# A hybrid attention layer on one core: attention cut into steps that a queue hands out between the pieces of the following projections, and nine instead of seven chunks of the first modulation piece on TensorE

## The chip, the cores and the metric

The kernel runs on one core of one Trainium2 chip. The time is device microseconds (us) for one execution of the whole program. Before the change it is 1295.29 us, the median of 3 runs (1293.72 to 1296.18). The profile comes from one further execution of the same program.

## What is computed

One decoder layer for 256 tokens of width 2048, all in fp32. Two attention branches run on the same normalised input `h`, and their outputs are gated and merged:

```python
mod = einsum('bd,de->be', silu(c), w_ada) + b_ada          # shift, scale, gate
h = rms_norm(x, g_pre) * (1 + scale) + shift
proj = einsum('bsd,de->bse', h, w_in)                      # 2048 -> 20032
q_mla, kv_a, z_mla, qkv_dil, z_dil, gl_mla, gl_dil = split(proj)
a = mla_branch(q_mla, kv_a, positions, g_kv, w_kv_b) * silu(z_mla)    # 16 heads, causal
bb = dilated_branch(qkv_dil, positions) * silu(z_dil)                 # 8 heads, 3 key groups
merged = sigmoid(gl_mla) * (a @ w_mla_proj) + sigmoid(gl_dil) * (bb @ w_dil_proj)
out = x + gate * rms_norm(merged @ w_o, g_post)
```

## The kernel before

**Projections.** Every projection is cut into column groups 512 wide (`group`, or `visit` for the first thirteen). A group walks the 2048 rows of its weight in chunks of 256 rows: `load_split` fetches a chunk of 512 KB into one of 8 `raw` buffers, ScalarE (ACT) casts it to a high part `whi`, VectorE (DVE) subtracts to get the low part `wlo` (4 buffers of each), and `multiply` issues 12 matmuls of 128x512 in fp32r: `whi` with the high part of `h`, `whi` with its low part, `wlo` with its high part, each for two rows of tiles and two token tiles. A whole group is 8 chunks.

**The head.** `h` can't be made before shift and scale are known. `ada_steps(0)` computes them for the first 384 channels out of 16 chunks of `w_ada`; `ROW_K` names the chunks that TensorE multiplies (into `row`, copied out by ACT, turned into columns by `pt_row`), the others are added up on DVE (tile `ada`, line L193). `keep_busy` issues matmuls into `idle`, whose result nobody reads. `finish` sums `ada` over the partitions (`pt_ada`), makes `colmul` and `colsh`, and calls `make_h`, which writes `hTh` and `hTl`, the high and low parts of `h`, for each 128 channels.

**Attention.** `dil_attention(quad)` treats 4 of the 8 dilated heads, one after the other; the body of the loop over `f`, `pr` and `h` treats the 16 latent heads. For each head: transposes of queries and keys on TensorE (`pt_qk`), copied out by ACT (`qk`); scores (`s_D`, `s_M`); mask and maximum on DVE, exponential on ACT (`sm`); transposes of the probabilities (`pt_p`), copied out by ACT (`pT`); the product with the values (`pv`); scaling on DVE. `transpose_split` then makes the operand of the next projection. In the code an attention stands as one block in front of the projections that follow it.

**What sets the order.** The code is traced, and a list scheduler fixes the order of each engine's instructions when the program is built; what stands earlier in the code has the higher priority, and where its inputs are not ready by the scheduler's own costs, later work is drawn ahead. So the projections behind an attention block already stand between its parts. On the chip every engine keeps that order and waits where an input is late. PSUM holds 2 accumulators and 4 smaller buffers (tag `b`) in these stages.

**In the trace,** an fp32 matmul that is no transpose stands as two instructions; a transpose and an fp32r matmul as one.

Of the kernel before, what the change touches and what calls it, by code (L numbers as in the profile page):

```python
# [9 lines left out]
F32 = mybir.dt.float32  # L10
F32R = mybir.dt.float32r
# [28 lines left out]
ROW_K = (1, 3, 5, 7, 9, 11, 13)  # L40
# [33 lines left out]
def hybrid_block(ctx: ExitStack, tc: tile.TileContext, x, c, positions, w_ada, b_ada, g_pre, g_post,  # L74
# [77 lines left out]
    def ada_steps(pi):  # L152
# [23 lines left out]
        def one(k0, kn):  # L176
# [23 lines left out]
        def finish():  # L200
# [12 lines left out]
            if pi == 0:  # L213
                keep_busy(acc[:, 0, :])
# [230 lines left out]

    def softmax(srcs, mask, n, scale, name):
# [39 lines left out]
    def dil_attention(quad):  # L486
        bb = slot([P, 2, 512], f"bb{quad}")
        for h in range(4):
            hs = slice(h * P, (h + 1) * P)
            nm = f"D{quad}{h}"  # L490
            qk = [qk_t([dil[0, g, quad][:, t, hs] for t in range(2)],
                       [dil[1, g, quad][:, t, hs] for t in range(2)], f"{nm}{g}") for g in range(3)]
            for t in range(2):
                nk = (t + 1) * P
                n = 3 * nk
                srcs = []
                for gs in ((0, 1, 2),) if t == 0 else ((0, 1), (2,)):
                    sc = tp_tile([P, len(gs) * nk], f"s_{nm}{t}{gs[0]}")
# [4 lines left out]
                sm, rl = softmax(srcs, md1 if t else md0, n, SC_DIL, f"{nm}{t}")  # L503
                pT = probs_t(sm, n // P, f"{nm}{t}")
                nb = 3 * (t + 1)
                pv = tp_tile([P, P], f"pv_{nm}{t}")
                for b in range(nb):
                    g, kt = divmod(b, t + 1)
                    T.matmul(pv, pT[:, b, :], dil[2, g, quad][:, kt, hs],  # L509
                             start=b == 0, stop=b == nb - 1)  # L510
                V.scalar_tensor_tensor(bb[:, t, hs], pv, rl, zd[quad][:, t, hs],
                                       op0=ALU.mult, op1=ALU.mult)
        bbT_h[quad] = slot([P, 4, S], f"bbTh{quad}", F32R)
        bbT_l[quad] = slot([P, 4, S], f"bbTl{quad}", F32R)
        transpose_split(bb, bbT_h[quad], bbT_l[quad], f"bb{quad}")
# [45 lines left out]
    for pi in range(len(PIECES)):  # L561
# [11 lines left out]
        for i, gi in enumerate(todo):  # L573
# [17 lines left out]
    for g in range(1, 3):  # L591
        for s in range(3):
# [3 lines left out]
            A.copy(dil[s, g, 1], acc)  # L596
    dil_rope(1)
    dil_attention(1)


    ssk = cp.tile([P, 2], F32, tag="ssk", name="ssk")
    for t in range(2):
        j = sp.tile([P, 768], F32, tag="sm", name=f"junk_kv{t}")
        A.activation(j[:, 0:512], kva[:, t, 0:512], AF.Square, accum_out=ssk[:, t:t + 1])
    rk = cp.tile([P, 2], F32, tag="rk", name="rk")
    rsqrt_mean(rk, ssk, 512, "rk")
    for t in range(2):
        V.tensor_scalar(kva[:, t, 0:512], kva[:, t, 0:512], rk[:, t:t + 1], None, op0=ALU.mult)
    ckv_h = slot([P, 4, S], "ckvh", F32R)
    ckv_l = slot([P, 4, S], "ckvl", F32R)  # L610
    for k in range(4):
        pt = tp_tile([P, 2, P], f"pt_ckv{k}")
        for t in range(2):
            T.transpose(pt[:, t, :], kva[:, t, k * P:(k + 1) * P], ident)
        h = sp.tile([P, S], F32, tag="h", bufs=H_BUFS, name=f"ckv{k}")
        V.tensor_scalar(h, pt.rearrange("p t n -> p (t n)"), gkv[:, k:k + 1], None, op0=ALU.mult)
        split(ckv_h[:, k, :], ckv_l[:, k, :], h)
    ckv = Opd([ckv_h], [ckv_l])

# [12 lines left out]
    V.memset(kz, 0.0)
    flat = pt.rearrange("p t n -> p (t n)")
    A.copy(kph, flat)
    for h in range(2):
        r, o = slice(h * 64, (h + 1) * 64), slice((1 - h) * 64, (2 - h) * 64)
        V.tensor_tensor(kpl[r, h, :], flat[r], kph[r].bitcast(F32), ALU.subtract)
        V.tensor_copy(kpl[o, h, :], kz[o])
# [4 lines left out]
    mqs, mq_done = {}, 0  # L643
    for f in range(4):
# [4 lines left out]
        for pr in range(2):  # L649
            j = 2 * f + pr  # L650
            gate_some(KC // UK // 2)
            while mq_done < 384 * (j + 1):
                acc = group(hT, win, KC, mq_done, 512, f"mq{mq_done // 512}")
                for i in range(mq_done // 384, (mq_done + 511) // 384 + 1):
# [9 lines left out]
            qp = sp.tile([P, 2, P], F32, tag="h", bufs=H_BUFS, name=f"qp{j}")  # L664
            rope(qp.rearrange("p t (h r) -> p (t h) r", r=64),
                 mq.rearrange("p t (h e) -> p (t h) e", e=192)[:, :, 128:192], cosMm, sinMm, 64, f"q{j}")
            pt = tp_tile([P, 2, P], f"pt_qp{j}")
            for t in range(2):
                T.transpose(pt[:, t, :], qp[:, t, :], ident)

            qst = sp.tile([P, 2, S], F32R, tag="qst", name=f"qst{j}")
            flat = pt.rearrange("p t n -> p (t n)")
            for h in range(2):
                r, o = slice(h * 64, (h + 1) * 64), slice((1 - h) * 64, (2 - h) * 64)
                A.copy(qst[r, h, :], flat[r])
                V.tensor_tensor(qst[o, h, :], flat[r], qst[r, h, :].bitcast(F32), ALU.subtract)
            for h in range(2):
                nm = f"M{j}{h}"
                qk = qk_t([mq[:, t, h * 192:h * 192 + P] for t in range(2)],
                          [kv[:, t, h * S:h * S + P] for t in range(2)], nm)  # L680
                sc = tp_tile([P, 3 * P], f"s_{nm}")
                for t in (1, 0):
                    nk = (t + 1) * P
                    o = 0 if t else S
                    T.matmul(sc[:, o:o + nk], qk[:, 0, t * P:(t + 1) * P], qk[:, 1, 0:nk],  # L685
                             start=True, stop=False)
                    qr = qst[:, h, t * P:(t + 1) * P]
                    T.matmul(sc[:, o:o + nk], qr, kph[:, 0:nk], start=False, stop=False)
                    T.matmul(sc[:, o:o + nk], qr, kpl[:, h, 0:nk], start=False, stop=True)
                sm = sp.tile([P, 768], F32, tag="sm", name=f"sm_{nm}")  # L690
                st = sp.tile([P, 8], F32, tag="stm", bufs=4, name=f"st_{nm}")
                for t in (1, 0):
                    nk = (t + 1) * P
                    o = 0 if t else S
                    V.tensor_tensor_reduce(sm[:, o:o + nk], sc[:, o:o + nk], mm[t], 1.0, -3e38,
                                           op0=ALU.add, op1=ALU.max, accum_out=st[:, t:t + 1])
                V.tensor_scalar(st[:, 2:4], st[:, 0:2], -SC_MLA, None, op0=ALU.mult)
                for t in (1, 0):
                    nk = (t + 1) * P
                    o = 0 if t else S  # L700
                    A.activation(sm[:, o:o + nk], sm[:, o:o + nk], AF.Exp, bias=st[:, 2 + t:3 + t], scale=SC_MLA,
                                 accum_out=st[:, 4 + t:5 + t])
                V.reciprocal(st[:, 6:8], st[:, 4:6])
                pT = probs_t(sm, 3, nm)
                pv = tp_tile([P, 2, P], f"pv_{nm}")
                vs = [kv[:, t, h * S + P:(h + 1) * S] for t in range(2)]
                T.matmul(pv[:, 1, :], pT[:, 0, :], vs[0], start=True, stop=False)
                T.matmul(pv[:, 1, :], pT[:, 1, :], vs[1], start=False, stop=True)
                T.matmul(pv[:, 0, :], pT[:, 2, :], vs[0], start=True, stop=True)
                hs = slice((2 * pr + h) * P, (2 * pr + h + 1) * P)  # L710
                for t in range(2):
# [107 lines left out]
```

## Time and profile before

| | |
|---|---|
| median of 3 runs | 1295.29 us (1293.72 to 1296.18) |
| the profiled execution's own time | 1292.55 us |
| its span in the trace | 1290.8 us |
| TensorE matmuls (PE) | busy 1265.4 us, 98% of the span, 6093 instructions |
| TensorE weight loads (PEld) | busy 1043.6 us, 81% |
| VectorE (DVE) | busy 821.1 us, 64% |
| ScalarE (ACT) | busy 601.0 us, 47% |
| DMA | 275 MB, mean 213 GB/s |

The stages, by the time from the span's start: the head to 36 us; the first thirteen groups in seven rounds to about 364 us; the attention of the first dilated quad (350 to 416 us) with six further groups behind it to 533 us; the attention of the second quad (to 590 us); the latent heads among their projections (590 to 902 us); gates and output projections to 1280 us; the tail. Matmuls are pipelined and their ends in the trace are modelled, so a start is read more surely than an end.

### The profile page before, as it was taken

To read this page: it belongs to the slowest core of one execution; us is meant where nothing else is said; L and a number is where in the kernel's file an instruction comes from. 1 tells how busy PE (TensorE), PEld (TensorE's weight loads), DVE (VectorE), ACT (ScalarE), POOL (GpSimd) and SP (SyncE) were. 2 spreads that over 40 slices of the span, in tenths; PEclk is the share of its full clock that TensorE was granted. 3 is DMA by queue.
4 is the path that set the end of the run, shared out by engine and by line. 5 is a ranking of instruction groups with operands and counts; after the bars stand their busy time and mean duration, and the time that the engine had idled before them with its cause. 6 is when DMAs were issued, how large, how long until landed. Compare 5 with 4: busy or idle time off the path is not lost.

```text
span 1290.8 us, 16449 instructions
## 1 busy us (share of the span) xinstructions
PE 1265.4 (98%) x6093; PEld 1043.6 (81%) x6093; DVE 821.1 (64%) x1203; ACT 601.0 (47%) x776; POOL 0.2 (0%) x4
## 2 busy tenths in 40 slices
PE   6999999999999999999999999999999999999997
PEld 3788888888888888888778888788888888888886
DVE  4888888896974445449666585675444444565545
ACT  3655334433365444455545555555444444433442
POOL 0000000000000000000000000000000000000000
PEclk9999999999999999999999999999999999999998
DMA  9999988986552766526768495674666666666751
GB/s 331 328 308 335 301 283 286 293 292 204 175 148 82 196 194 190 168 72 209 228 212 255 121 323 157 207 250 124 195 194 195 196 194 192 197 218 195 249 159 66
DMA packets 158172, 275.01 MB, mean 213 GB/s; under 512 B 9542, under 2 KB 46860, under 8 KB 158092
## 3 DMA queue, kind: packets, MB, share of 16 engines
q1 hardware_dynamic: 156276, 268.43, 66.5%
q10 hardware_dynamic: 1816, 5.53, 1.1%
q8 instruction: 48, 0.79, 0.2%
q14 instruction: 32, 0.26, 0.1%
HBM read 271.83 MB, written 2.10 MB: 212 GB/s over the span
## 4 chain that ended last, share of the span: by engine, by line
PE 94%; DVE 2%; DMA 1%; ACT 1%; issue 1%; DVEq 0%; SPq 0%; ACTq 0%
PE acc_d L264 30%; PE acc_mq L264 10%; PE acc_gd L264 7%; PE acc_ym L264 7%; PE acc_gm L264 7%; PE acc_zm L264 6%; PE acc_o L264 6%; PE acc_zd L264 3%; PE acc_yd L264 3%; PE acc_kv L264 3%; PE acc_kva L264 2%; PE pv_D L509 1%; PE s_D L500 1%; PE s_M L685 1%; PE pt_pD L466 1%
## 5 line engine op out<-in xcount | busy, mean ns | idle before, releaser
L253 ACT CAST whi_d<-raw_d 128x1024 fp32r<-128x1024 f32 (+1 forms) x156 | 152.8, 987 | 179.0 <-PE acc_d L264 145.3
L254 DVE TENSOR_TENSOR wlo_d<-raw_d,whi_d 128x1024 fp32r<-128x1024 f32 (+1 forms) x156 | 176.5, 1139 | 65.1 <-ACT whi_d L253 63.2
L264 PE MATMUL acc_d<-whi_d,hTl 128*128 128x512 f32 x576 | 159.4, 392 | 0.5 <-DVE hTl L231 0.5
L264 PE MATMUL acc_d<-whi_d,hTh 128*128 128x512 f32 x576 | 157.9, 392 | 1.4 <-DVE d L555 1.4
L264 PE MATMUL acc_d<-wlo_d,hTh 128*128 128x512 f32 x576 | 156.9, 390 | 0.0
L264 PEld LDWEIGHTS acc_d<-whi_d,hTh 128*128 128x128 f32 x576 | 107.2, 188 | 24.0 <-issue 1.8
L264 PEld LDWEIGHTS acc_d<-whi_d,hTl 128*128 128x128 f32 x576 | 107.8, 188 | 22.9 <-DVE hTl L231 1.0
L264 PEld LDWEIGHTS acc_d<-wlo_d,hTh 128*128 128x128 f32 x576 | 108.0, 188 | 22.3
L193 DVE SCALAR_TENSOR_TENSOR ada<-raw_a,ccol,ada 128x512 f32<-128x512 f32 (+1 forms) x98 | 79.4, 810 | 15.9 <-DMA raw_a<-in_w_ada 14.8
L254 DVE TENSOR_TENSOR wlo_mq<-raw_mq,whi_mq 128x1024 fp32r<-128x1024 f32 x48 | 58.6, 1222 | 24.4 <-ACT whi_mq L253 20.4
L253 ACT CAST whi_mq<-raw_mq 128x1024 fp32r<-128x1024 f32 x48 | 50.4, 1052 | 47.0 <-PE acc_mq L264 20.5
L254 DVE TENSOR_TENSOR wlo_gm<-raw_gm,whi_gm 128x1024 fp32r<-128x1024 f32 x32 | 39.2, 1225 | 45.4 <-ACT whi_gm L253 45.4
L254 DVE TENSOR_TENSOR wlo_gd<-raw_gd,whi_gd 128x1024 fp32r<-128x1024 f32 x32 | 39.2, 1224 | 32.4 <-ACT whi_gd L253 30.5
L254 DVE TENSOR_TENSOR wlo_ym<-raw_ym,whi_ym 128x1024 fp32r<-128x1024 f32 x32 | 39.1, 1223 | 32.1 <-ACT whi_ym L253 30.6
L253 ACT CAST whi_ym<-raw_ym 128x1024 fp32r<-128x1024 f32 x32 | 33.8, 1055 | 51.0 <-PE acc_ym L264 37.6
L253 ACT CAST whi_gm<-raw_gm 128x1024 fp32r<-128x1024 f32 x32 | 33.8, 1055 | 49.6 <-PE acc_gm L264 43.9
L254 DVE TENSOR_TENSOR wlo_o<-raw_o,whi_o 128x1024 fp32r<-128x1024 f32 x28 | 34.3, 1225 | 35.3 <-ACT whi_o L253 35.3
L264 PE MATMUL acc_mq<-wlo_mq,hTh 128*128 128x512 f32 x192 | 52.9, 393 | 0.0
L264 PE MATMUL acc_mq<-whi_mq,hTl 128*128 128x512 f32 x192 | 52.9, 394 | 0.0
L253 ACT CAST whi_gd<-raw_gd 128x1024 fp32r<-128x1024 f32 x32 | 33.7, 1053 | 40.5 <-PE acc_gd L264 20.4
L254 DVE TENSOR_TENSOR wlo_zm<-raw_zm,whi_zm 128x1024 fp32r<-128x1024 f32 x32 | 39.2, 1224 | 20.8 <-ACT whi_zm L253 18.2
L264 PE MATMUL acc_mq<-whi_mq,hTh 128*128 128x512 f32 x192 | 52.0, 392 | 0.0
(281 smaller groups left out, 2350.3 us busy)
## 6 DMA issues: line engine op xcount, KB each, us to landing
raw_d<-in_w_in SPq DMA_DIRECT2D x132, 512.0 KB, 4.6
raw_mq<-in_w_in SPq DMA_DIRECT2D x48, 512.0 KB, 4.6
raw_a<-in_w_ada SPq DMA_DIRECT2D x80, 256.0 KB, 4.7
raw_zm<-in_w_in SPq DMA_DIRECT2D x32, 512.0 KB, 4.4
raw_g<-in_w_ada SPq DMA_DIRECT2D x32, 512.0 KB, 4.2
raw_gd<-in_w_in SPq DMA_DIRECT2D x32, 512.0 KB, 4.4
raw_gm<-in_w_in SPq DMA_DIRECT2D x32, 512.0 KB, 3.8
raw_ym<-in_w_mla_proj SPq DMA_DIRECT2D x32, 512.0 KB, 3.7
```

The costliest lines, as they stand in the source:

```text
L193: V.scalar_tensor_tensor(flat, w, ccol[:, kk:kk + 1], flat, op0=ALU.mult, op1=ALU.add)
L253: A.copy(whi[:, :m], raw[:, :m])
L254: V.tensor_tensor(wlo[:, :m], raw[:, :m], whi[:, :m].bitcast(F32), ALU.subtract)
L264: T.matmul(acc[:, t, :n], opd.get(part, k0 + k, t), wt[:, k * n:(k + 1) * n], start=start and ph == 0 and k == 0, stop=stop and ph == 2 an ...
L466: T.transpose(pt[:, b, :], sm[:, (b0 + b) * P:(b0 + b + 1) * P], ident)
L500: T.matmul(sc[:, i * nk:(i + 1) * nk], qk[g][:, 0, t * P:(t + 1) * P], qk[g][:, 1, 0:nk], start=True, stop=True)
L509: T.matmul(pv, pT[:, b, :], dil[2, g, quad][:, kt, hs], start=b == 0, stop=b == nb - 1)
L685: T.matmul(sc[:, o:o + nk], qk[:, 0, t * P:(t + 1) * P], qk[:, 1, 0:nk], start=True, stop=False)
```

## The change

The attention functions become lists of closures. A list `side` holds them, and `run` takes one off (`tick`) after every chunk. `dil_steps` gives 16 steps for a quad (`s1` query and key transposes of a head, `s2` scores and softmax, `s3` probability transposes, `s4` the product with the values) in an order that overlaps neighbouring heads, and 2 steps for `transpose_split`; `kv_steps` gives 6 for the compressed keys, `mla_steps` 9 for two latent heads. What an instruction computes stays the same. In the head `ROW_K` has nine chunks instead of seven, `keep_busy` runs for chunks 12, 13 and 14 instead of 14 and 15, and the one in `finish` is gone.

```diff
-ROW_K = (1, 3, 5, 7, 9, 11, 13)
+ROW_K = (1, 2, 3, 5, 6, 7, 9, 10, 11)
...
-                if pi == 0 and kk > ROW_K[-1]:
+                if pi == 0 and ROW_K[-1] < kk < KC - 1:
                     keep_busy(v[:, k, 0, :])
...
                 make_h(a + lo, a + hi)
-            if pi == 0:
-                keep_busy(acc[:, 0, :])
...
+    side = []
+
+    def tick():
+        if side:
+            side.pop(0)()
+
     def run(acc, opd, w, a, b, c0, n, name):
 
         for k, kn in chunks(a, b, n):
             whi, wlo = load_split(w, k, kn, c0, n, f"{name}_{k}")
             multiply(acc, opd, whi, wlo, k, kn, n, k == a, k + kn == b)
+            tick()
...
-    def dil_attention(quad):
-        bb = slot([P, 2, 512], f"bb{quad}")
-        for h in range(4):
+    def dil_steps(quad):
+
+        bb = []
+        kept = {}
+
+        def s1(h):
...
+        def s3(h):
+            kept[h] = [(probs_t(sm, 3 * (t + 1), f"D{quad}{h}{t}"), rl) for t, (sm, rl) in enumerate(kept[h])]
...
+        order = [(s1, 0), (s2, 0), (s1, 1), (s3, 0), (s2, 1), (s4, 0), (s1, 2), (s3, 1), (s2, 2), (s4, 1),
+                 (s1, 3), (s3, 2), (s2, 3), (s4, 2), (s3, 3), (s4, 3)]
+        return ([lambda f=f, h=h: f(h) for f, h in order]
+                + transpose_steps(lambda: bb[0], bbT_h, bbT_l, quad, "bb"))
...
                 dil_rope(0)
-                dil_attention(0)
+                side.extend(dil_steps(0))
+                side.extend(kv_steps())
     A.activation(zd[1], zd[1], AF.Silu)
...
+    while side:
+        tick()
     dil_rope(1)
-    dil_attention(1)
...
+    side.extend(dil_steps(1))
...
+        return [rot] + [lambda f=f, h=h: f(h) for f in (s1, s2, s3, s4) for h in range(2)]
+
     for f in range(4):
...
+            side.extend(mla_steps(j, mq, kv, zm, av))
+        side.extend(transpose_steps(lambda av=av: av, aT_h, aT_l, f, "av"))
```

How this moves instructions is seen in the built programs. First TensorE in the attention of the first dilated quad, third head, before (`acc_d` is a projection, `pt_pD` the probability transposes, `pv_D` the product with the values, `s_D` the scores):

```order
L264 MATMUL acc_d_3598<-whi_d_2_3619,hTh_294 128x512 x4
L264 MATMUL acc_d_3598<-whi_d_2_3619,hTl_295 128x512
L466 MATMUL pt_pD_3310<-tid,sm_D_3303 128x128 x3
L264 MATMUL acc_d_3598<-whi_d_2_3619,hTl_295 128x512 x3
L509 MATMUL pv_D_3315<-d_205,pT_D_3309 128x128
L509 MATMUL pv_D_3315<-d_206,pT_D_3309 128x128
L509 MATMUL pv_D_3315<-d_207,pT_D_3309 128x128
L500 MATMUL s_D_3320<-qkD_3283 128x256
L500 MATMUL s_D_3320<-qkD_3290 128x256
L500 MATMUL s_D_3323<-qkD_3297 128x256
L264 MATMUL acc_d_3598<-wlo_d_2_3620,hTh_294 128x512 x4
```

The same place after the change, from the end of the chunk ahead of the probability transposes of that head:

```order
L262 MATMUL acc_d_3449<-wlo_d_6_3563,hTh_603 128x512 x4
L487 MATMUL pt_pD_3579<-tid,sm_D_3472 128x128 x3
L487 MATMUL pt_pD_3585<-tid,sm_D_3483 128x128 x3
L487 MATMUL pt_pD_3590<-tid,sm_D_3483 128x128 x3
L262 MATMUL acc_d_3449<-whi_d_8_3597,hTh_1458 128x512 x4
L262 MATMUL acc_d_3449<-whi_d_8_3597,hTl_1459 128x512 x4
L262 MATMUL acc_d_3449<-wlo_d_8_3598,hTh_1458 128x512 x4
L525 MATMUL s_D_3613<-qkD_3544 128x128
L525 MATMUL s_D_3613<-qkD_3551 128x128
L525 MATMUL s_D_3613<-qkD_3558 128x128
```

Three projection matmuls stood between the probability transposes and the product that needs them; now whole chunks of 12 stand between steps, and the step behind the transposes is another head's.

Then DVE in the head, before: the last three chunks that it adds up (`ada`), the two additions that wait for TensorE's row (`cols`, L173 and L174), and the first of the small operations behind them.

```order
L193 SCALAR_TENSOR_TENSOR ada_215<-raw_a_12_260,ccol,ada_215 128x768
L193 SCALAR_TENSOR_TENSOR ada_215<-raw_a_14_278,ccol,ada_215 128x768
L193 SCALAR_TENSOR_TENSOR ada_215<-raw_a_15_283,ccol,ada_215 128x768
L173 TENSOR_TENSOR cols<-cols,pt_row 128x3
L174 TENSOR_TENSOR cols<-cols,pt_row 128x3
L208 TENSOR_TENSOR adasc_288<-pt_ada_216,cols 128x1
```

After:

```order
L193 SCALAR_TENSOR_TENSOR ada_218<-raw_a_12_277,ccol,ada_218 128x768
L193 SCALAR_TENSOR_TENSOR ada_218<-raw_a_13_282,ccol,ada_218 128x768
L173 TENSOR_TENSOR cols<-cols,pt_row 128x3
L174 TENSOR_TENSOR cols<-cols,pt_row 128x3
L193 SCALAR_TENSOR_TENSOR ada_218<-raw_a_14_287,ccol,ada_218 128x768
L193 SCALAR_TENSOR_TENSOR ada_218<-raw_a_15_292,ccol,ada_218 128x768
```

The wait for the row now stands ahead of the last two chunks. A little further on the same queue, before:

```order
L211 TENSOR_TENSOR colsh<-pt_ada_216,cols 128x1
L231 SCALAR_TENSOR_TENSOR hTl_295<-h_296,colsh,hTh_294 128x256
L209 SCALAR_TENSOR_TENSOR colmul<-adasc_288,cols 128x1
L254 TENSOR_TENSOR wlo_d_0_326<-raw_d_0_323,whi_d_0_325 128x1024
L231 SCALAR_TENSOR_TENSOR hTl_295<-h_305,colsh,hTh_294 128x256
L229 SCALAR_TENSOR_TENSOR h_314<-xT_101,colmul,rstdT 128x256
```

After:

```order
L211 TENSOR_TENSOR colsh<-pt_ada_219,cols 128x1
L252 TENSOR_TENSOR wlo_d_0_331<-raw_d_0_328,whi_d_0_330 128x1024
L229 SCALAR_TENSOR_TENSOR hTl_302<-h_303,colsh,hTh_301 128x256
L229 SCALAR_TENSOR_TENSOR hTl_302<-h_312,colsh,hTh_301 128x256
L209 SCALAR_TENSOR_TENSOR colmul<-adasc_295,cols 128x1
L252 TENSOR_TENSOR wlo_d_2_349<-raw_d_2_346,whi_d_2_348 128x512
L227 SCALAR_TENSOR_TENSOR h_321<-xT_101,colmul,rstdT 128x256
```

Both weight splits (`wlo_d`) now stand ahead of the third `h`.

## Rows read from the trace of the kernel before

**Rows 1.** Stretch, length; busy (count) of PE, PEld, DVE, ACT, POOL; granted clock; DMA.

```profile
350.00:420.00 70.00, 69.81 (x399) 57.73 (x398) 43.52 (x90) 41.67 (x63) 0.00 (x0) 1.00 0.41 120
420.00:530.00 110.00, 110.00 (x487) 91.09 (x486) 57.25 (x70) 46.77 (x46) 0.00 (x0) 1.00 0.69 195
530.00:590.00 60.00, 59.75 (x349) 48.76 (x349) 28.83 (x80) 33.37 (x59) 0.00 (x0) 1.00 0.34 100
590.00:910.00 320.00, 317.42 (x1559) 260.90 (x1557) 211.15 (x358) 172.83 (x256) 0.00 (x0) 1.00 0.66 211
```

**Rows 2.** The same view of projection matmuls (L264) alone: PE, PEld, clock, DMA.

```profile
350.00:420.00 70.00, 46.69 (x187) 32.47 (x186) 1.00 0.41 120
530.00:590.00 60.00, 35.32 (x127) 22.45 (x127) 1.00 0.34 100
590.00:910.00 320.00, 283.19 (x1173) 215.97 (x1173) 1.00 0.66 211
```

**Rows 3.** Pieces of the chain that ended last: start us, us, what.

```profile
374.15 1.35 PE pv_D L509 x12
382.87 1.30 PE s_D L500 x6
...
1011.71 87.04 PE acc_gm L264 x384
...
1148.74 0.89 PE pt_m L442 x8
...
1269.69 5.78 PE acc_last L264 x48
```

**Rows 4.** Weight loads' longest wait, 530 to 910 us: total, times, longest.

```profile
PEld pt_pM L466 <- ACT sm_M L701: 4.8, 10, 1.3
```

**Rows 5.** Timeline of one dilated head's softmax: start, us, engine, line, operation.

```profile
382.71 1.46 PE L500 MATMUL s_D<-qkD 128*128 128x256 f32 x6
383.77 0.69 DVE L453 CUSTOM_DVE_ANT_0 sm_D<-s_D,msk 128x512 f32<-128x512 f32 x1 [0.51 <-PE s_D L500]
...
384.44 1.06 ACT L253 CAST whi_d<-raw_d 128x1024 fp32r<-128x1024 f32 x1 [2.55 <-PE acc_d L264]
...
386.55 0.82 PE L466 MATMUL pt_pD<-tid,sm_D 128*128 128x128 f32 x6
386.57 1.21 DVE L254 TENSOR_TENSOR wlo_d<-raw_d,whi_d 128x1024 fp32r<-128x1024 f32 x1
...
389.74 1.56 ACT L477 COPY qkD<-pt_qkD 128x512 f32<-128x512 f32 x3 [1.75 <-PE pt_qkD L475]
```

**Rows 6.** The page's costliest group of casts: busy, mean ns, idle before and what ended it.

```profile
L253 ACT CAST whi_d<-raw_d 128x1024 fp32r<-128x1024 f32 (+1 forms) x156 | 152.8, 987 | 179.0 <-PE acc_d L264 145.3
```

**Rows 7.** Timeline of the head.

```profile
25.50 1.45 PE L186 MATMUL row<-raw_a,ccol 128*1 128x384 f32 x4 [0.66 <-DMA raw_a<-in_w_ada]
...
26.60 2.07 DVE L193 SCALAR_TENSOR_TENSOR ada<-raw_a,ccol,ada 128x768 f32<-128x768 f32 x2 [1.09 <-DMA raw_a<-in_w_ada]
26.98 0.79 ACT L167 COPY rowp<-row 1x768 f32<-1x768 f32 x1 [13.15 <-PE row L186]
...
27.82 1.49 PE L171 MATMUL pt_row<-ones,rowp 1*128 1x1 f32 x12 [0.88 <-ACT rowp L167]
...
30.97 0.50 PE L206 MATMUL pt_ada<-ones,ada 128*128 128x1 f32 x4
...
31.33 0.89 PE L150 MATMUL idle<-ada,tid 128*128 128x384 f32 x2
...
35.66 0.48 DVE L229 SCALAR_TENSOR_TENSOR h<-xT,colmul,rstdT 128x256 f32<-128x256 f32 x1
35.79 0.73 PE L264 MATMUL acc_d<-whi_d,hTl 128*128 128x512 f32 x2 [0.52 <-DVE hTl L231]
...
36.17 0.51 ACT L230 ACTIVATE hTh<-h,colsh 128x256 fp32r<-128x256 f32 x1 [2.15 <-DVE h L229]
```

**Rows 8.** The view of Rows 1 behind the last matmul, which starts before 1281.3 us.

```profile
1284.00:1287.00 3.00, 0.00 (x0) 0.00 (x0) 2.77 (x4) 0.00 (x0) 0.00 (x0) 0.50 0.21 86
```

More of the change, by code (lines that the diff above doesn't have):

```diff
@@ L444, in transpose_split, with transpose_steps, step @@
             split(hi[:, 2 * hp:2 * hp + 2, :], lo[:, 2 * hp:2 * hp + 2, :], v)
+    def transpose_steps(src, dst_h, dst_l, i, name):
+        def step(hp):
+            if hp == 0:
+                dst_h[i] = slot([P, 4, S], f"{name}h{i}", F32R)
+                dst_l[i] = slot([P, 4, S], f"{name}l{i}", F32R)
+            pt = tp_tile([P, 2, 2, P], f"pt_{name}{i}{hp}")
+            for b in range(2):
+                for t in range(2):
+                    cc = (hp * 2 + b) * P
+                    T.transpose(pt[:, b, t, :], src()[:, t, cc:cc + P], ident)
+            v = pt.rearrange("p b t n -> p b (t n)")
+            split(dst_h[i][:, 2 * hp:2 * hp + 2, :], dst_l[i][:, 2 * hp:2 * hp + 2, :], v)
+        return [lambda hp=hp: step(hp) for hp in range(2)]
     def softmax(srcs, mask, n, scale, name):
@@ L502, in dil_attention, with s4 @@
                     srcs.append(sc)
-                sm, rl = softmax(srcs, md1 if t else md0, n, SC_DIL, f"{nm}{t}")
-                pT = probs_t(sm, n // P, f"{nm}{t}")
+                res.append(softmax(srcs, md1 if t else md0, 3 * nk, SC_DIL, f"D{quad}{h}{t}"))
+            kept[h] = res
+        def s3(h):
+            kept[h] = [(probs_t(sm, 3 * (t + 1), f"D{quad}{h}{t}"), rl) for t, (sm, rl) in enumerate(kept[h])]
+        def s4(h):
+            if not bb:
+                bb.append(slot([P, 2, 512], f"bb{quad}"))
+            hs = slice(h * P, (h + 1) * P)
+            for t, (pT, rl) in enumerate(kept[h]):
@@ L505, in dil_attention @@
                 nb = 3 * (t + 1)
-                pv = tp_tile([P, P], f"pv_{nm}{t}")
+                pv = tp_tile([P, P], f"pv_D{quad}{h}{t}")
                 for b in range(nb):
                     g, kt = divmod(b, t + 1)
[L509 to L512, printed above, removed]
@@ new lines, in dil_steps, with kv_steps, norm, turn @@
+        return ([lambda f=f, h=h: f(h) for f, h in order]
+                + transpose_steps(lambda: bb[0], bbT_h, bbT_l, quad, "bb"))
+    ckv_h, ckv_l = [], []
+    ckv = Opd(ckv_h, ckv_l)
+    kp = cp.tile([P, 2, P], F32, tag="kp", name="kp")
+    kph = cp.tile([P, S], F32R, tag="kph", name="kph")
+    kpl = cp.tile([P, 2, S], F32R, tag="kpl", name="kpl")
+    def kv_steps():
+        def norm():
+            ssk = cp.tile([P, 2], F32, tag="ssk", name="ssk")
+            junk = slot([P, 2, 512], "junk_kv")
+            for t in range(2):
+                A.activation(junk[:, t, :], kva[:, t, 0:512], AF.Square, accum_out=ssk[:, t:t + 1])
+            rk = cp.tile([P, 2], F32, tag="rk", name="rk")
+            rsqrt_mean(rk, ssk, 512, "rk")
+            for t in range(2):
+                V.tensor_scalar(kva[:, t, 0:512], kva[:, t, 0:512], rk[:, t:t + 1], None, op0=ALU.mult)
+                rope(kp[:, t:t + 1, 0:64], kpe[:, t:t + 1, :], cosM[:, t, 0:1, :], sinM[:, t, 0:1, :], 64, f"kp{t}")
+            V.tensor_copy(kp[:, :, 64:128], kp[:, :, 0:64])
+        def turn(k):
+            if k == 0:
+                ckv_h.append(slot([P, 4, S], "ckvh", F32R))
+                ckv_l.append(slot([P, 4, S], "ckvl", F32R))
+            pt = tp_tile([P, 2, P], f"pt_ckv{k}")
+            for t in range(2):
+                T.transpose(pt[:, t, :], kva[:, t, k * P:(k + 1) * P], ident)
+            h = sp.tile([P, S], F32, tag="h", bufs=H_BUFS, name=f"ckv{k}")
+            V.tensor_scalar(h, pt.rearrange("p t n -> p (t n)"), gkv[:, k:k + 1], None, op0=ALU.mult)
+            split(ckv_h[0][:, k, :], ckv_l[0][:, k, :], h)
+        def key():
+            pt = tp_tile([P, 2, P], "pt_kp")
+            for t in range(2):
+                T.transpose(pt[:, t, :], kp[:, t, :], ident)
+            kz = sp.tile([P, S], F32, tag="h", bufs=H_BUFS, name="kz")
+            V.memset(kz, 0.0)
+            flat = pt.rearrange("p t n -> p (t n)")
+            A.copy(kph, flat)
+            for h in range(2):
+                r, o = slice(h * 64, (h + 1) * 64), slice((1 - h) * 64, (2 - h) * 64)
+                V.tensor_tensor(kpl[r, h, :], flat[r], kph[r].bitcast(F32), ALU.subtract)
+                V.tensor_copy(kpl[o, h, :], kz[o])
+        return [norm] + [lambda k=k: turn(k) for k in range(4)] + [key]
@@ L663, in hybrid_block @@
             A.copy(kv, acc)
[L664 to L711, printed above, removed]
-                    V.scalar_tensor_tensor(av[:, t, hs], pv[:, t, :], st[:, 6 + t:7 + t], zm[:, t, hs],
-                                           op0=ALU.mult, op1=ALU.mult)
@@ L728, in hybrid_block @@
         part.append(sg)
+    while side:
+        tick()
     sgm = []
```

115 lines of the change are left out of this document (68 added, 47 removed).

## The prediction

> **What bounds the kernel now.** Start with the page's busy line: TensorE matmuls fill 98% of the span, VectorE 64%, ScalarE 47%. So TensorE is the bound, and the only time to be won without taking work away is time in which its work goes slower than it could. Busy time does not show that. In the stretch of the first quad's attention PE is busy 69.81 of 70 us, in one without attention 110.00 of 110 [rows 1]. So I count instructions and price them at the rate at which they run where nothing is waited for.
>
> The prices come from the chain, where a piece is printed with its length and count [rows 3]: 87.04 us for 384 projection matmuls 512 wide is 0.2267 each; 0.89 for 8 transposes is 0.111; 1.35 for 12 fp32 instructions 128 wide is 0.1125; 1.30 for 6 of 256 is 0.217; 5.78 for 48 fp32r ones 256 wide is 0.1204. Check: the 487 instructions between 420 and 530 us, all projections, cost 110.4 at 0.2267, and took 110.
>
> First quad, 350 to 420 us: 399 instructions, 187 of them projections [rows 1, 2]. The other 212 follow from the code: 92 transposes (48 for queries and keys, 36 for probabilities, 8 for `bb`), 96 fp32 instructions 128 wide, 24 of 256. Of the 187, 24 are the narrower `kva` (an estimate by their width: 0.134). The sum: 163 x 0.2267 = 36.95, 24 x 0.134 = 3.2, 92 x 0.111 = 10.2, 96 x 0.1125 = 10.8, 24 x 0.217 = 5.2, together 66.35. **3.7 us are lost.**
>
> Second quad, 530 to 590: 349 less 127 is 222 (the 212 and ten transposes of the compressed keys). 28.8 + 102 x 0.111 + 10.8 + 5.2 = 56.1 of 60. **3.9 lost.**
>
> Latent heads, 590 to 910: 1559 less 1173 is 386: 162 transposes (18.0), 96 for the values (10.8), 128 for the scores (32 each of fp32 256 and 128 wide, fp32r 256 and 128 wide: 6.9 + 3.6 + 3.9 + 3.6). With 1173 x 0.2267 = 265.9 that is 312.7 of 320. **7.3 lost.** Together 14.9 us, 1.2% of the time.
>
> What they are lost to stands among the waits: probability transposes wait for the exponential, 4.8 us in ten waits, the longest 1.3 [rows 4]. One case in full [rows 5]: scores issued from 382.71, the first maximum on DVE at 383.77, the transposes at 386.55. The scheduler had put only 11 projection matmuls (2.5 us) between scores and transposes, about the length of the chain, so any split of weights in the queues of DVE or ACT (1.2 and 1.06) shows as a wait.
>
> The Trainium skill (Perfetto Trace Analysis, Identifying the Most-Contended Engine) holds that matmul occupancy is a poor measure because the instructions are pipelined, and takes the busy share of weight loads in its place. The rows agree with its first half: 69.81 of 70 us busy hides 3.7 lost. By its second half the shares are 82.5, 81.3 and 81.5% in the three stretches against 82.8% between 420 and 530, and the loss would be 0.3 + 1.1 + 4.9 = 6.3 us, not 14.9. I go by the count, since the mix of sizes, not only waiting, moves that share.
>
> **The change, part by part.**
>
> *Attention as steps.* Nothing is added or taken away on TensorE, so its priced work is equal. What moves is the distance between a step and the one that needs its result. A chunk is 12 x 0.2267 = 2.72 us. In the built order of a quad, `s2` (scores) to `s3` (transposes) of a head is two chunks and the neighbour's `s1`: 5.4 + 1.3 = 6.8 us. The chain that must fit is the 2.5 us of [rows 5]; with two splits of 1.2 ahead of it on DVE it is 5.0. `s3` to `s4` is two chunks and an `s2`, 7.4 us, against copies of about 0.5 each. `s1` to `s2` is the tightest, one chunk of 2.7 against three copies (1.56) behind one cast (1.06): 2.6. The last `s3` to `s4` of a quad also has one chunk. Among the latent heads each such pair has at least one chunk and mostly two (5.4 us) against a maximum, an exponential and one split. So nearly every wait named above loses its reason. What stays: ten one-chunk places at about 0.1, and the change between kinds of matmul at some 120 places, which at 0.02 (within the price of a transpose, so not measured alone) is 2.4. I take 3.4 us as staying, 11.5 won. Bounds: all 14.9 from above; from below nothing, since each engine's queue could bring the waits back.
>
> *The splits.* A step's copies and exponentials stand in ACT's and DVE's queues before the casts and splits of later chunks, and TensorE waits for those. Cover: ACT's casts are held up by TensorE's release of the four buffers (145.3 of 179.0 us of idle time ahead of `whi_d`, [rows 6]), so they run about three chunks, 8 us, ahead. Load: at a chunk and a step every 4.3 us DVE has a split and by my estimate about 0.8 of attention (a maximum takes 0.69), ACT a cast and about 1.2 (copies of 0.52) [rows 5]. I cost it at nothing. Without that cover the price would be what a step holds the queue, 1 to 2 us.
>
> *The compressed keys' steps* move from the second quad's end to the groups before it: ten transposes, 1.1 us, unchanged in price, and DVE's small operations into a stretch where it is busy 57 of 110 us [rows 1]. Nothing.
>
> *Nine chunks.* [rows 7] give the head before: the last `row` chunk starts at 25.50 and takes 1.45, its copy 0.79 at 26.98, `pt_row` 27.82, two idle matmul pairs, `pt_ada` at 30.97, though DVE has its last chunk added at 28.67. After: a chunk of `row` costs about 1.3 on TensorE and the chunks land about 1.05 apart (both estimates: four matmuls take 1.45, and DVE adds two chunks in 2.07 as they land), so I put the end of the ninth near 25.4; the copy ends near 26.3, `pt_row` near 27.9, 1.3 earlier. Three idle pairs of 0.9 follow instead of two (1.72 for two), so `pt_ada` comes near 30.6, 0.4 earlier. DVE now has the wait for `pt_row` ahead of its last two chunks: 28.2 + 2 x 1.02 = 30.3 instead of 28.67, just in time. The pair taken out of `finish` (31.33) frees perhaps 0.2. Against it: both weight splits (1.2 and 0.7) now stand ahead of the third `h` on DVE; it starts near 36.1 instead of 35.66, its cast ends near 37.2, and the first projection needs it there at 37.15 before the change. The sum is 0.1 to the bad, which I take as 0. Bounds: 0.9 won (0.4 + 0.2 and an `h` that is in time), 1.2 lost (one split in the open).
>
> **Sum.** 1292.55 (the profiled execution) - 11.5 + 0 = 1281.05. The median of the runs lies 2.74 above that execution, so 1283.8, say **1284 us**.
>
> **The rivals.**
>
> *Only part comes back.* The short waits of 0.1 to 0.2 may belong to the change of kinds rather than to late inputs; then only those above half a microsecond go, and 4 to 7 us are won: 1288 to 1291. For it: most of the ten waits behind 4.8 us are short [rows 4]. Against: they are named with a releaser. By the skill's measure above it would be 1289. Chance 0.18.
>
> *No change.* The scheduler already fills the gaps, the new order meets its waits in the queues of DVE instead, and 1294 to 1297 is measured. Against: the distances above are twice the chain. Chance 0.06.
>
> *Slower: the splits come late.* ACT and DVE keep their order, so an exponential that stands there waiting for its maximum holds up the casts behind it. One cast late beyond its 8 us stops TensorE. It decides from 0.6 us for each of the 24 heads (14.9 / 24); at 1 us a head the time is 1295 + 24 - 15 = 1304. For it: DVE in the latent stretch is busy 211 of 320 us and has its gate sums there. Against: [rows 6]. Chance 0.05.
>
> *Slower by the clock.* With one idle pair gone TensorE could stand still long enough in the head to lose its clock; behind the last matmul it is granted 0.50 [rows 8], against 1.00 everywhere else after the head's start. A few us of projections at 1.2 instead of 2.4 GHz cost about 2. It alone would not turn the sign: 1286. Chance 0.03, within the forecast's range. The skill (TensorE: Matmul & The Clock Gate, Why this matters for your kernels) warns of gaps between bursts of matmuls in the same sense.
>
> **How the numbers follow.** Forecast 0.71 with its own range 1280.5 to 1287.5; part 0.18; none 0.06; slower 0.05. The range that leaves out two in ten: 1280 (all of 14.9 and a little of the head) to 1290.5, in the middle of the part case. About 0.2% (2.6 us) is what a measurement can tell from no change: faster 0.88, same 0.07, slower 0.05.
>
> **What would show it.** Right: between 350 and 910 us the same count takes about 11 us less; the wait of `pt_pM` for `sm_M` is gone from the list; whole chunks of 12 stand between steps in the timeline; the first full run of projections starts within 1 us of 36; no waits of projections for `whi` or `wlo`. Wrong: such waits appear, or the lost time in the three stretches stays above 8 us, or the granted clock is below 1.00 in the head.

## The result and the profile after

The change takes 1281.49 us (median of 4 executions, 1280.25 to 1282.87), the kernel before 1294.97 (4 executions, 1293.72 to 1296.18): a ratio of 0.9897, 95% interval 0.9885 to 0.9910. The profiled execution of the change took 1281.44 us with a span of 1279.7, 11.1 below the span of before.

Where the 11.1 us came from is read between marks that both kernels have: the one transpose `pt_pos` of the last round, and the first matmul of `acc_ym`. Timeline of PE before (start, us, engine, line, operation):

```profile
323.34 0.22 PE L376 MATMUL pt_pos<-tid,posf 2*128 2x2 f32 x1
1098.58 1.07 PE L264 MATMUL acc_ym<-whi_ym,aTh 128*128 128x512 f32 x4
```

The same of the change:

```profile
324.99 0.22 PE L382 MATMUL pt_pos<-tid,posf 2*128 2x2 f32 x1
1087.48 1.07 PE L262 MATMUL acc_ym<-whi_ym,avh 128*128 128x512 f32 x4
```

Between the marks, where all attention lies, 775.24 us became 762.49: **12.75 won**. Up to the first mark the change is **1.65 later**. Behind the second nothing changed (192.2 us to the end of the span in both). 12.75 - 1.65 = 11.1.

**The attention.** The stretches of [rows 1] after the change (same columns):

```profile
350.00:420.00 70.00, 70.00 (x402) 60.87 (x401) 45.98 (x100) 41.30 (x63) 0.00 (x0) 1.00 0.49 139
590.00:910.00 320.00, 320.00 (x1602) 268.69 (x1601) 196.98 (x340) 172.98 (x257) 0.00 (x0) 1.00 0.66 202
```

PE starts 43 more instructions in the same 320 us (1559 before). The waits of PE's weight loads before, from 340 to 930 us, beside [rows 4] (total us, times, longest):

```profile
PEld pv_D L509 <- ACT pT_D L467: 5.1, 15, 0.4
...
PEld pt_pD L466 <- ACT sm_D L457: 4.5, 15, 0.4
PEld s_M L685 <- ACT qkM L477: 2.5, 14, 0.2
...
PEld s_M L688 <- DVE qst L676: 1.8, 3, 1.3
```

All nine groups of that list make 25.3 us, more than the 12.75 won, so a listed wait is not lost time in full. After the change one is left in the same stretch:

```profile
PEld s_D L525 <- ACT qkD L498: 0.2, 1, 0.2
```

It stands at 361.94 us, in the first head, where one chunk lies between the copies and the scores: the place that the prediction called the tightest.

The timeline of the third head's scores shows why, beside [rows 5]:

```profile
389.67 2.13 PE L525 MATMUL s_D<-qkD 128*128 128x128 f32 x12
390.09 1.22 DVE L252 TENSOR_TENSOR wlo_d<-raw_d,whi_d 128x1024 fp32r<-128x1024 f32 x1 [1.60 <-ACT whi_d L251]
391.24 0.55 DVE L474 CUSTOM_DVE_ANT_0 sm_D<-s_D,msk 128x384 f32<-128x384 f32 x1
391.45 1.28 PE L262 MATMUL acc_d<-whi_d,hTh 128*128 128x512 f32 x4
...
393.33 0.94 ACT L478 ACTIVATE sm_D<-sm_D,st_D 128x768 f32<-128x768 f32 x1
393.48 1.08 PE L262 MATMUL acc_d<-wlo_d,hTh 128*128 128x512 f32 x4
...
394.40 2.17 PE L543 MATMUL pv_D<-d,pT_D 128*128 128x128 f32 x18
...
396.32 1.17 PE L262 MATMUL acc_d<-whi_d,hTh 128*128 128x512 f32 x4
...
397.34 0.85 PE L262 MATMUL acc_d<-whi_d,hTl 128*128 128x512 f32 x3
```

While DVE and ACT work on this head (391.24 to 394.3), PE multiplies a whole chunk and then the values of the second head; a split of 1.22 us ahead of the maximum delays nothing.

**The head.** Here the granted clock fell. Windows of the change (length; PE, PEld, DVE, ACT, POOL; granted clock; DMA):

```profile
27.00:28.00 1.00, 1.00 (x10) 0.98 (x10) 0.00 (x0) 0.00 (x0) 0.00 (x0) 0.91 1.04 385
28.00:31.00 3.00, 2.94 (x5) 1.33 (x5) 2.17 (x4) 1.04 (x1) 0.00 (x0) 0.50 1.08 356
31.00:32.00 1.00, 1.00 (x6) 0.60 (x4) 0.00 (x0) 0.00 (x0) 0.00 (x0) 0.88 1.06 330
32.00:34.00 2.00, 1.37 (x12) 1.20 (x11) 1.51 (x8) 0.51 (x1) 0.00 (x0) 1.00 0.93 289
34.00:35.00 1.00, 0.99 (x5) 0.56 (x5) 0.95 (x4) 0.80 (x2) 0.00 (x0) 0.82 1.05 346
35.00:38.00 3.00, 2.96 (x7) 1.85 (x8) 2.43 (x6) 0.75 (x3) 0.00 (x0) 0.50 0.97 320
```

The profiled execution of before has 1.00 throughout:

```profile
27.00:40.00 13.00, 11.27 (x55) 8.34 (x56) 9.50 (x24) 5.96 (x9) 0.00 (x0) 1.00 0.96 324
```

Timeline of the change at the same place, against [rows 7]:

```profile
25.67 0.79 ACT L167 COPY rowp<-row 1x768 f32<-1x768 f32 x1 [11.82 <-PE row L186]
26.51 1.54 PE L171 MATMUL pt_row<-ones,rowp 1*128 1x1 f32 x12 [0.88 <-ACT rowp L167]
27.98 4.01 PE L150 MATMUL idle<-raw_a,tid 128*128 128x384 f32 x6
28.23 2.07 DVE L193 SCALAR_TENSOR_TENSOR ada<-raw_a,ccol,ada 128x768 f32<-128x768 f32 x2
31.84 0.50 PE L206 MATMUL pt_ada<-ones,ada 128*128 128x1 f32 x4
36.95 0.48 DVE L227 SCALAR_TENSOR_TENSOR h<-xT,colmul,rstdT 128x256 f32<-128x256 f32 x1
```

DVE's sum is ready at 30.30, as forecast; but behind a wait of 0.88 and twelve tiny matmuls the clock falls to 0.50 (1.2 GHz), the six idle matmuls take 4.01 us instead of the 2.7 forecast, and `pt_ada`, queued behind them, comes at 31.84 instead of 30.6. Behind the small matmuls of `pt_ada` it falls again, from 34.8 to 38 us, under the first projections.

### The profile page after: what moved, and what is told of

Its sections match the earlier page's. It is cut to its first block, busy times and chain, and to the rows that moved or that the text cites. A ratio compares the mean times of both kernels' runs of the same rounds, so it can differ in the third digit from the quotient of the medians.

```text
span 1279.7 us, 16445 instructions
## 1 busy us (share of the span) xinstructions
PE 1260.7 (99%) x6101; PEld 1050.0 (82%) x6101; DVE 814.8 (64%) x1201; ACT 601.9 (47%) x778; POOL 0.2 (0%) x4
## 4 chain that ended last, share of the span: by engine, by line
PE 98%; DVE 1%; DMA 0%; ACT 0%; issue 0%; DVEq 0%; SPq 0%; ACTq 0%
PE acc_d L262 31%; PE acc_mq L262 10%; PE acc_zm L262 7%; PE acc_gd L262 7%; PE acc_ym L262 7%; PE acc_gm L262 7%; PE acc_o L262 6%; PE acc_kv L262 3%; PE acc_yd L262 3%; PE acc_zd L262 3%; PE acc_kva L262 2%; PE pv_D L543 1%; PE s_D L525 1%; PE s_M L722 1%; PE row L186 1%; PE pt_pD L487 1%
## 5 line engine op out<-in xcount | busy, mean ns | idle before, releaser
L252 DVE TENSOR_TENSOR wlo_gd<-raw_gd,whi_gd 128x1024 fp32r<-128x1024 f32 x32 | 39.2, 1224 | 37.3 <-ACT whi_gd L251 37.3
L262 PE MATMUL acc_mq<-whi_mq,hTh 128*128 128x512 f32 x192 | 55.2, 409 | 0.0
L251 ACT CAST whi_zm<-raw_zm 128x1024 fp32r<-128x1024 f32 x32 | 33.6, 1051 | 39.5 <-PE acc_zm L262 12.5
```

What stands on the lines that cost most here:

```text
L251: A.copy(whi[:, :m], raw[:, :m])
L252: V.tensor_tensor(wlo[:, :m], raw[:, :m], whi[:, :m].bitcast(F32), ALU.subtract)
L262: T.matmul(acc[:, t, :n], opd.get(part, k0 + k, t), wt[:, k * n:(k + 1) * n], start=start and ph == 0 and k == 0, stop=stop and ph == 2 an ...
```

## The experiments

"Stretch" is the time between the two marks. The expectations count it from an earlier mark, which adds 105.3 us in every kernel. The clock is the mean granted clock over an execution. Before was run again beside each; its medians there were 1295.57, 1293.57, 1295.36 and 1295.90.

| kernel | stretch, us | median, us (range; executions) | mean clock | ratio to before, interval |
|---|---|---|---|---|
| before | 775.24 | 1295.36 (1292.45 to 1298.50; 17) | 0.992 to 0.998 | |
| the change | 762.49 | 1281.49 (1280.25 to 1282.87; 4) | 0.995 to 0.996 | 0.9897 [0.9885, 0.9910] |
| head alone | 775.62 | 1294.28 (1292.44 to 1295.48; 12) | 0.994 to 0.997 | 0.9995 [0.9985, 1.0004] |
| steps alone | 762.56 | 1279.90 (1279.78 to 1283.44; 5) | 0.994 to 0.998 | 0.9896 [0.9880, 0.9912] |
| in order | 763.74 | 1283.78 (1282.93 to 1285.17; 4) | 0.992 to 0.995 | 0.9913 [0.9896, 0.9930] |
| two per chunk | 762.43 | 1280.50 (1279.95 to 1284.20; 4) | 0.993 to 0.997 | 0.9896 [0.9879, 0.9913] |
| no idle | 762.59 | 1281.81 (1281.21 to 1282.14; 5) | 0.994 to 0.995 | 0.9910 [0.9894, 0.9926] |
| steps, fill | 762.55 | 1280.18 (1279.93 to 1280.31; 4) | 0.997 to 0.998 | 0.9898 [0.9882, 0.9913] |
| change, fill | 762.58 | 1280.10 (1279.95 to 1280.81; 4) | 0.997 to 0.998 | 0.9898 [0.9883, 0.9914] |
| two buffers | 763.31 | 1290.94 (1288.73 to 1293.97; 10) | 0.993 to 0.996 | 0.9977 [0.9963, 0.9990] |
| at once | 784.81 | 1303.21 (1302.98 to 1305.08; 4) | 0.988 to 0.991 | 1.0059 [1.0044, 1.0073] |
| half chunks | 771.56 | 1290.80 (1289.32 to 1292.01; 6) | 0.994 to 0.997 | 0.9964 [0.9950, 0.9978] |
| before, fill | 774.79 | 1292.73 (1292.24 to 1294.22; 11) | 0.997 to 0.998 | 0.9982 [0.9972, 0.9992] |
| at once, late kv | 769.11 | 1288.92 (1288.49 to 1290.29; 5) | 0.993 to 0.995 | 0.9948 [0.9931, 0.9965] |

**The two halves of the change.** The head alone, in the kernel before:

```diff
-ROW_K = (1, 3, 5, 7, 9, 11, 13)
+ROW_K = (1, 2, 3, 5, 6, 7, 9, 10, 11)
-                if pi == 0 and kk > ROW_K[-1]:
+                if pi == 0 and ROW_K[-1] < kk < KC - 1:
-            if pi == 0:
-                keep_busy(acc[:, 0, :])
```

> The kernel before with the head of the change alone: nine chunks of the row on TensorE, idle matmuls at chunks 12, 13 and 14, none in finish. The prediction (head costs 0, bounds 0.9 won and 1.2 lost): the time of before within 0.5 us. Rival, read from the trace of the change (probability sums delayed from 30.97 to 31.84 us behind three idle pairs, second low part of h from 35.26 to 35.9 behind a weight split): 1.0 to 1.6 us slower than before, with the same losses as before in the attention stretches.

The steps alone, which is the change with these lines put back:

> The change with the head of before: seven chunks, idle matmuls at chunks 14 and 15 and in finish, all attention still handed out step by step. If the head of the change costs nothing, the time is that of the change within 0.5 us. If it costs 1.0 to 1.6 us, this kernel is faster than the change by that much: about 1280.1 us, a span of 1278.4, some 12.4 below the span of before.

The stretch is the steps' alone: 762.56 with them, 775.62 without. The head alone is not slower than before (0.9995); its profiled execution is 1.3 us longer, and its clock fell there from 33.9 to 37.3 us. The steps alone fall into two bunches, 1279.8 to 1279.9 at a mean clock of 0.997 to 0.998 and 1283.4 at 0.994. Before does much the same: of its 17 executions in the group of the table, 6 lie between 1292.45 and 1293.21 at 0.997 to 0.998 and 11 between 1295.08 and 1298.50 at 0.992 to 0.994. The head alone shows no such gap: its times run from 1292.44 to 1295.48 while the clock goes from 0.997 to 0.994. So a time says little about the head unless the clock is read beside it.

**How much distance the steps need.** In order, and in order with a step per half chunk:

```diff
-        order = [(s1, 0), (s2, 0), (s1, 1), (s3, 0), (s2, 1), (s4, 0), (s1, 2), (s3, 1), (s2, 2), (s4, 1),
-                 (s1, 3), (s3, 2), (s2, 3), (s4, 2), (s3, 3), (s4, 3)]
+        order = [(f, h) for h in range(4) for f in (s1, s2, s3, s4)]
-        return [rot] + [lambda f=f, h=h: f(h) for f in (s1, s2, s3, s4) for h in range(2)]
+        return [rot] + [lambda f=f, h=h: f(h) for h in range(2) for f in (s1, s2, s3, s4)]
```

> The change with the steps of a head one after the other instead of overlapped with the neighbour's, so that one chunk (2.72 us) instead of 6.8 us stands between scores and probability transposes, with as many steps and as many changes between kinds of matmul. Theory of distance: the chain behind the scores takes 2.5 to 5 us, so waits of the probability transposes for the exponential come back in the trace, 0.2 to 1 us in each of 24 heads, and the time rises by 3 to 10 us over the change. Rival, that the gain comes from whole chunks in place of finely mixed kinds of matmul: within 1 us of the change.

For half chunks the `tick()` of `run` goes, and `multiply` has, behind each matmul pair:

```diff
+                if nk == 2 and 2 * ph + k in (2, 5):
+                    tick()
```

> The change with the steps of a head one after the other, as in the run in order, and one step after every half chunk (6 matmuls, 1.36 us). Whole chunks between steps cost 1.2 us with this order. Theory of distance: 1.36 us no longer covers the 2.5 us chain, so 3 to 9 us come back in the stretch from the first rounds to the last projections (867.8 us in the change), with waits of pt_p for sm and of pv for pT. Rival, that any projections between the steps are enough: within 2 us of it.

With one chunk between the steps of a head the stretch is 1.25 us longer than in the change; 3 to 10 was too much; 2.72 us of projections is just longer than the 2.5 us chain, which fits. (Its median is 2.3 longer; in its profiled execution the clock also stayed at 0.50 from 28 to 41 us.) With half a chunk it is 9.07 longer, and the waits of [rows 4] are back. Weight loads' waits, half chunks, 340 to 930 us:

```profile
PEld pt_pM L488 <- ACT sm_M L737: 7.3, 20, 0.8
PEld pv_M L750 <- ACT pT_M L489: 4.0, 14, 0.3
PEld pt_pD L488 <- ACT sm_D L479: 3.6, 11, 0.4
```

In order, a whole chunk apart:

```profile
PEld pv_M L749 <- ACT pT_M L488: 1.4, 3, 0.6
PEld pt_pD L487 <- ACT sm_D L478: 0.8, 3, 0.3
```

Two steps per chunk (a second `tick()` in `run`):

> The change with two steps handed out after each chunk: half as many places where projections and attention alternate, and between scores and probability transposes one chunk and one step of a neighbour (about 4 us) instead of 6.8. Theory of distance: 4 us still covers the 2.5 us chain and mostly one split ahead of it; 0 to 3 us slower than the change, with a few waits of pt_p for sm. Rival, that alternation itself costs about 0.1 us at each place (some 110 places): 3 to 6 us faster than the change.

762.43 against 762.49: in all nothing is lost or won. But some waits are back. The list of weight loads' waits from 340 to 930 us makes 3.3 us, against 0.2 in the change and 3.1 in order; among them:

```profile
PEld s_D L526 <- ACT qkD L499: 0.6, 3, 0.3
...
PEld pt_pM L488 <- ACT sm_M L738: 0.4, 2, 0.2
```

So the rival's 0.1 us a place is refuted, but a small price of the alternation could be hidden behind these waits. The starts in the trace give an estimate of it. Behind the 18 instructions of `pv_D` at 394.40 (change, above) the projections start after 1.92 us instead of 2.03 at 0.1125 each, and the first four of them take 1.02 us instead of 0.91: the two nearly cancel. Between the marks TensorE goes back to projections at 116 places in the change. Summed over them, the first projection matmuls take 10.6 us more than the usual distance between starts and the attention instructions ahead of them 8.7 less: 1.9 us, 0.016 a place. With two steps per chunk it is 72 places, 6.4 and 5.3, so 1.1 us. By this estimate about 0.8 us was won with fewer alternations and lost again in waits.

The overlapped order without the chunks, by a loop `while side: tick()` behind each `side.extend`. In the first form the steps of the compressed keys also come ahead of the last sums of `kva`, so this part of the computation is changed:

> The change with every list of steps handed out at once where it is put into the queue, so that the overlapped order of the steps stays and the whole chunks between them go; what stands between is again what the scheduler draws ahead, for the dilated heads almost nothing. Theory of distance: a neighbour's step (1 to 1.4 us) against a chain of 2.5 us leaves waits of the probability transposes for the exponential and of scores for copies; the time from the first rounds to the last projections (880.5 us before, 867.8 after) goes back to 876 to 884, the median to 1289 to 1297. Rival, that the overlapped order alone wins the time: 868 to 870 there.

> The run with lists handed out at once, but the steps of the compressed keys stay in the queue and come after the first thirteen groups; in the first form they stood ahead of the last sums of kva, which cost waits of 3.8 and 4.6 us of its own (and gave other results). Theory of distance: the stretch from the first rounds to the last projections takes 876 to 884 us (867.8 in the change, 880.5 before), the median is 1289 to 1297. Rival, that the overlapped order alone wins the time: 868 to 870 there.

The first form cost 22.3 us, with waits that its own misplaced steps caused, among them:

```profile
PE pt_ckv L578 <- DVE kva L568: 4.6, 1, 4.6
PE acc_zd L262 <- DVE kva L636: 3.8, 1, 3.8
```

The second lands between both theories: 769.11, 6.6 above the change and 6.1 below before. Its weight loads' waits say where:

```profile
PEld s_M L728 <- DVE qst L714: 3.9, 4, 1.1
PEld pt_pM L487 <- ACT sm_M L741: 3.2, 11, 0.4
...
PEld pt_pD L487 <- ACT sm_D L478: 1.3, 4, 0.5
```

The latent heads still wait for `sm` and `qst`; the dilated heads' wait for `sm` is down from 4.5 us before to 1.3. All listed waits of the dilated heads go from 11.8 to 3.0 us, those of the latent heads from 13.3 to 12.1. So the overlapped order, with only the projections that the scheduler draws ahead, does about half of it, mostly among the dilated heads, and the chunks do the rest.

**The splits.** Two buffers in place of four:

```diff
-W_BUFS = 4
+W_BUFS = 2
```

> The change with two instead of four buffers for the split weights, so that casts and splits run one chunk ahead of TensorE instead of three. The prediction costs the splits at nothing because of their lead of 8 us, and 1 to 2 us a step without it. If so, waits of projections for whi or wlo appear in the trace between 350 and 910 us and the time rises by 15 to 60 us (some 70 steps that hold ACT or DVE, 0.2 to 0.9 us each), with no such waits in the stretch without attention. Rival, that a lead of one chunk is enough: within 2 us of the change.

The stretch is 0.8 us longer, and between 340 and 930 us no wait of a projection is listed. For the time as a whole both forecasts failed: the median is 9.5 us above the change's and the span of the profiled execution 7.6. Of the 7.6, 4.9 lie between the first `acc_zd` and the first mark, 0.8 in the stretch and 2.9 behind the second mark, less 1.0 in the head. From 76 to 325 us, where DVE also adds up modulation chunks, it is busy 205.75 of 249 us; from 325 to 930 us it is busy 378.34 of 605. Of the PE waits over the whole span:

```profile
PE acc_kva L262 <- DVE wlo_kva L252: 1.2, 2, 0.8
PE acc_zd L262 <- ACT whi_zd L251: 1.1, 1, 1.1
```

So a lead of one chunk covers the splits where attention stands. That the deeper lead pays where DVE is loaded is how I read these waits; they are 2.3 of the 4.9 us, and where the rest and the 2.9 go stays open.

**The clock in the head.** No idle matmuls (the `keep_busy` call of `one` is dropped):

> The change without any idle matmuls in the head. Theory of the clock, from the traces (in the profiled execution of the change the granted clock falls from 1.00 to 0.50 at 27.9 us, behind 0.88 us of waiting for the row's copy and twelve tiny matmuls, and again at 34.8; where the clock of an execution is 0.005 lower its time is 3 us longer): without idle matmuls it falls in every execution and stays low for longer, and the median is 1 to 4 us above that of the change. Rival, that the three idle pairs only hold up the probability sums: the sums come 1 us earlier and the median is 0.5 to 1 us below that of the change.

Filling: one more pair while TensorE waits for the row's copy, and one behind each block of channels in `finish` (behind the first two only, in the version with nine chunks), put into the steps alone, the change and the kernel before:

```diff
                     if kk == ROW_K[-1]:
+                        keep_busy(v[:, k, 1, :])
                         rows_done()
...
                 make_h(a + lo, a + hi)
+                if pi == 0:
+                    keep_busy(acc[:, 0, :])
```

> Steps handed out as in the change, the head of before (seven chunks), with one more idle pair in the 0.88 us in which TensorE waits for the row's copy, and one behind each of the three channel blocks in finish instead of one in all. Theory of the clock: the granted clock stays at 1.00 through the head in nearly all executions, so that the times bunch near the shortest of the kernel with steps alone (1279.8 us) instead of spreading to 1283.4. Rival, that the spread has another cause: two bunches 3.5 us apart as there, or all 0.5 to 1 us longer through the added idle pairs.

> The change with its nine chunks and three idle pairs, one more idle pair while TensorE waits for the row's copy, and one behind each of the first two channel blocks in finish. Theory of the clock: the granted clock stays at 1.00 in nearly all executions; what is left against the kernel with seven chunks and the same filling is the price of nine chunks by itself, which the traces at full clock (first projection run in the head-only kernel 0.8 us behind before, in spite of a fall at 33.9) put at 0 to 1 us. Median 1279.5 to 1281. Rival, no effect of the filling: the change's 1281.5.

> The kernel before with the same added idle pairs in the head as the run with seven chunks and filling, and nothing else. Theory of the clock: its times bunch near the short bunch of before (1291.9 to 1292.9 us), at 1292.0 to 1292.9, and the bunch at 1295 to 1298 is gone; against it the steps alone are then worth 12.2 us. Rival, that the bunches belong to something outside the head: the same two bunches as before.

Without idle matmuls all five executions lost the clock (0.994 to 0.995), but the median is only 0.3 above the change, whose executions had lost it too (0.995 to 0.996): the theory was right on the clock and wrong on the price against the change (1 to 4 us). Against the change with filling, timed beside it, the price is 1.7 (1281.81 and 1280.10). The rival's gain did not show: the sums come earlier (30.32 us against 31.84), but what follows runs at 0.50 until 38.7. With filling no execution of any of the three kernels is below 0.997, and the bunches of the longest times are gone. Which of the two places needs the filling was not tried. Not all of the spread is the clock's: before with filling runs from 1292.24 to 1294.22 at 0.997 to 0.998, and in another group before took 1295.20 and 1295.75 at 0.997. Windows of the steps with fill:

```profile
27.00:40.00 13.00, 12.75 (x60) 8.93 (x60) 8.96 (x24) 6.09 (x9) 0.00 (x0) 1.00 0.97 329
```

The kernel before with filling alone is faster than before (0.9982) with nothing changed behind the head. The change with filling takes 1280.10 us, 1.4 less than the change. The two were not timed side by side and the change's own executions spread over 2.6 us, so that it is better is likely and not shown; what is shown is that its executions bunch within 0.9.

## Why the prediction was right, and which steps were not

**Forecast.** 1284 was forecast and 1281.49 measured, inside the range. The mechanism held: the waits of [rows 4] are gone, whole chunks stand between the steps, no projection waits for a split. One of the prediction's own signs of being wrong did come: the granted clock fell below 1.00 in the head.

**Attention, -11.5: measured -12.75.** What was held to stay (3.4 us) was over-sized: by the same count about 14.9 - 12.75 = 2.1 is left. The 2.4 put on the change between kinds of matmul is of the right size, 1.9 by the estimate above. The 1.0 put on ten one-chunk places did not show, since one wait of 0.2 is listed. The 12.75 itself is good to about 0.4: three profiles with the attention of before have stretches of 774.79 to 775.62. The distances were argued as a chain of up to 5 us against 6.8; a chunk of 2.72 already does nearly all of it, so the reason asked for more than was needed.

Weight loads fill 84.4% of 350 to 910 us after the change (472.56 of 560; 458.48 before, 81.9%). The Trainium skill (Perfetto Trace Analysis, Identifying the Most-Contended Engine) takes this share as one measure of TensorE's headroom. It moved the right way; the 12.75 won are twice the 6.3 that the prediction estimated by it, and the count by prices was nearer.

**Splits, 0: right,** for a wider reason than given. Three chunks of lead were named as the cover; one is enough in the stretch. The rival by which splits come late had the wrong place.

**Nine chunks, 0: right as work, wrong as time.** In the filled kernels the first `acc_zd` group starts at 74.86 us with nine chunks, 75.35 with seven, and 74.94 before: the work is even, as worked out. (At the first mark the filled nine are 0.94 later than before; 0.74 of that is one wait for a split, `wlo_kva` at 197.39 us, which the change does not have.) The 1.65 us lost in the profiled execution belong to the clock: the change's first `acc_zd` is at 76.57, 1.63 later than before. That was the rival with a chance of 0.03 and a price of 2: the price was right and the chance far too small, for all four executions of the change have a mean clock of 0.995 to 0.996. The cause it named, the idle pair that is gone from `finish`, fits the profiles: in all nine of kernels without a pair there (no idle among them) the clock is 0.50 from 35 to 36 us, and in all five with one (before, steps alone and the three filled) it is 1.00 from 27 to 42. The filled change tells the pairs from the nine chunks, since it has both and keeps the clock. But that pair is not enough: before, which has it, shows a mean clock of 0.996 or less in 35 of its 57 executions. None of those was profiled, so where they lose it is not known. What ended the loss is work in the wait for the row and between the blocks of `finish`, both together.

**The median lies 2.74 above the profiled execution: the step that failed.** I carried this over as a constant. It goes with the clock in the head: the profile of before happened to be an execution that kept it, and before with filling, which always kept it, has its median at 1292.73, beside the profile's 1292.55. The profile of the change had lost it, and its time is its median's (1281.44 and 1281.49). On the profiled executions the sum was 0.4 off (1281.05): 1.25 too little from attention against 1.65 too little cost in the head, two errors that cancel by luck. The offset is what put the forecast 2.5 us too high. The medians differ by 13.5 us: 12.75 from the steps, and the rest, by this reading, because the clock cost the change 1.65 and before 2.4 (1294.97 - 1292.55).

## What to carry to other kernels

Where a busy engine alternates between a dependent chain and free work, put at least as much free work between dependent steps as the chain on the other engines takes; here one chunk of 2.72 us against 2.5 won nearly everything, half a chunk less than a third (12.75 - 9.07 = 3.7 us). Overlapping neighbours in the chain wins about half (6.1 us) without such chunks, with only what the scheduler draws ahead. Before adding the offset between a profile and a median to a forecast, compare the mean granted clock of the executions: an offset may be a second mode of the kernel.

## What was not expected of the hardware

The granted clock in the head differs between executions of one program: 0.992 to 0.998 on average for before, with two bunches of times some 3 us apart, and none between 1293.21 and 1295.08 in the 17 executions of the table (in another group of 17, four lie there). In the change it fell from 1.00 to 0.50 behind a wait of 0.88 us and twelve tiny matmuls, and a few idle matmuls in the waits kept it at a mean of 0.997 or more in all 19 filled executions. The Trainium skill (TensorE: Matmul & The Clock Gate, Part 1) says that the monitor's window runs freely of the program, so that the point of a change varies from run to run; the two bunches agree with that, though no run here shows the window itself.
